# A first stage without a pool of its own on the right, with its first maxima moved and most of GpSimd's arithmetic on other engines

## The chip, the cores and the metric

The kernel runs on one core of a Trainium2 chip. The time is the device time of one launch in microseconds. TensorE multiplies matrices, VectorE, ScalarE and GpSimd work element by element, SyncE issues most of the DMAs. The kernel before takes 3284.41 us (median of three runs, 3281.88 to 3284.51).

## The reference, cut to what matters

Two layers work on 2048 tokens of width 1024, with 256 context tokens as a prefix for the first layer's keys and values. All of it is in float32.

```
h = modulate(x, shift, scale) @ w_in                 # 2464 columns: cq, ckv, kr, gates, qb, kb, vb
q_a = rms_norm(cq) @ w_uq ;  k_a, v_a = rms_norm(ckv) @ w_ukv ;  k_pe = rope(kr) ; q_pe = rope(...)
q_b, k_b = rope(rms_norm(qb)), rope(rms_norm(kb))    # 8 query heads over 2 key heads
o = softmax(q k^T * scale) v    for 8 + 8 heads, over 256 + 2048 keys
x = layer_norm(alpha * x + gate * (concat(o * silu(g)) @ w_out))
x = the second layer, a gated MLP that mixes tokens in chunks of 128, on x
```

## The kernel before, in words

Every product of two float32 matrices is made of three products of rounded halves: a value is cut into a high part (a rounded copy) and a low part (value minus copy), and high x high, low x high and high x low are added up in one bank (`mm3`, lines 187 to 189).

The kernel has three stages. `phase1` makes queries, keys, values and gates for all tokens and stores them in DRAM. `attention` goes through 16 heads in four groups of 512 queries each, in an order that is written out by hand. `phase3` makes the output projection and the second layer. This case is about `phase1` and its end.

`phase1` works in two halves: the first on the context (chunk -1) and chunks 0 and 1 of 512 tokens, the second on chunks 2 and 3. For each chunk `acts` loads the raw activations (line 107, two buffers named `xr`), modulates them on ScalarE (176), copies the high part on GpSimd (178) and subtracts the low part on VectorE (179). High and low parts lie in rings of nine buffers, where a chunk needs four of each. `weights` does the same for each weight tile: load (155), high part on GpSimd (158), low part on VectorE (159). The products then come in the order key B, value B, four query B, two compressed key/value (`C2`), keys A, values A, the rope part of the keys, three compressed queries (`C3`), and last the "uq" products that make the A queries, three weight tiles `s` of two blocks for two chunks each, every one with 9 products. Units of gate products, 24 products each, are strewn in between by a generator, `gate`; in the second half six of them are left for the end.

Around the products stand small chains. `halves` cuts the squares of a result in two (242 on ScalarE, 243 on GpSimd), `rnorm` sums them with a product (251), takes a root (253) and a reciprocal (254). `rope` multiplies by a cosine table on GpSimd (223), shuffles (224), multiplies by a sine table (225) and adds on VectorE (226). `put` cuts the result in two and stores it (217). `later_rows` computes the modulation rows of later stages on VectorE (273, 275), three pieces with each weight tile, from weights that go through the two `xr` buffers as well.

The tiles lie in a pool on the left (`sp`) and an early pool on the right (`ap`), which holds squares, tables, the context's activations, the accumulators of `later_rows`, the C2 and C3 units and the values' tiles. When the uq products are through, the early pool is closed and the attention's pool `kp` is opened in its place: two slots of keys (`k`), two of values (`v`), three of queries (`q`). Then the keys of head 0 and the first two query tiles are loaded (552), and `first_peaks` makes the maxima of the first scores: 18 products with their reductions (618, 622, 632, 635) for the first group and 10 for the second. After the 18, the row of maxima goes to DRAM (639) and comes back into a row of the query tile (552), which the first score product reads. These come amid the last gate units, in this way:

```
for i, _ in enumerate(gate):
    if half == 1 and i > 0:
        n = 9 if i < 3 else 5
        if i == 3:
            todo.pop()()          # the row of maxima comes back
        for f in todo[:n]: f()
```

In `phase1` the order on each engine is not the program's. The framework's planner goes through the instructions by priority (program order, but for those in `high_priority`) with modelled durations, gives every engine and every queue a fixed order, and puts in the waits. On the chip each engine then goes through its list in order, SyncE's list of DMA issues too.

## Time and profile before

| | |
|---|---|
| median of three runs | 3284.41 us |
| profiled execution | 3284.32 us, span 3282.5 us |
| TensorE busy | 3183.2 us (97%) |
| VectorE / ScalarE / GpSimd busy | 2501.8 / 1892.4 / 1623.6 us |
| first stage | up to about 680 us |
| mean granted clock of TensorE | 0.989 |

A busy TensorE is not TensorE at its peak, since the ends of products are modelled: a product of 512 columns is shown with 0.39 us, while such products start 0.23 us apart when they follow without a wait. The clock is given as the share of full speed that was granted.

### The profile page before, as it was taken

To read this page: it belongs to the slowest core of one execution; us is meant where nothing else is said; L and a number is where in the kernel's file an instruction comes from. 1 tells how busy PE (TensorE), PEld (TensorE's weight loads), DVE (VectorE), ACT (ScalarE), POOL (GpSimd) and SP (SyncE) were. 2 spreads that over 40 slices of the span, in tenths; PEclk is the share of its full clock that TensorE was granted. 3 is DMA by queue.
4 is the path that set the end of the run, shared out by engine and by line. 5 is a ranking of instruction groups with operands and counts; after the bars stand their busy time and mean duration, and the time that the engine had idled before them with its cause. 6 is when DMAs were issued, how large, how long until landed. Compare 5 with 4: busy or idle time off the path is not lost.

```text
span 3282.5 us, 40436 instructions
## 1 busy us (share of the span) xinstructions
PE 3183.2 (97%) x13698; PEld 2429.2 (74%) x13698; DVE 2501.8 (76%) x3685; ACT 1892.4 (58%) x3258; POOL 1623.6 (49%) x1359
## 2 busy tenths in 40 slices
PE   7999999989999999999999999999999999999998
PEld 4787677767777777777666666666788878888886
DVE  4947794578988888888999999998655764855746
ACT  3433342357777777777777777777444353353352
POOL 3312441259999999998888888874100100100000
PEclk9999999989999999999999999999999999999999
DMA  6455755543122221222111111112633533533322
GB/s 235 142 164 181 247 161 175 160 115 61 40 50 61 61 59 30 63 61 61 28 30 27 27 49 29 27 30 60 165 96 109 143 120 109 155 102 109 116 91 76
DMA packets 187056, 314.08 MB, mean 96 GB/s; under 512 B 53264, under 2 KB 79184, under 8 KB 184928
## 3 DMA queue, kind: packets, MB, share of 16 engines
q1 hardware_dynamic: 178558, 283.62, 30.6%
q0 software_dynamic: 8000, 27.81, 2.8%
q8 instruction: 108, 1.77, 0.3%
q14 instruction: 100, 0.82, 0.1%
q10 hardware_dynamic: 290, 0.07, 0.0%
HBM read 240.71 MB, written 70.73 MB: 95 GB/s over the span
## 4 chain that ended last, share of the span: by engine, by line
PE 52%; issue 11%; DMA 9%; POOL 6%; DVE 6%; ACT 2%; SPq 0%; POOLq 0%; ACTq 0%; DVEq 0%
PE s L603 14%; DMA NM<-nm 6%; PE ol L603 6%; PE oh L603 5%; PE m L603 5%; POOL sa L603 4%; PE acc L935 3%; PE acc L934 3%; PE acc L936 3%; PE acc L1031 3%; PE acc L1030 3%; PE acc L1029 3%; DVE pl L603 2%; DMA q<-NM 2%; PE ps L188 1%
## 5 line engine op out<-in xcount | busy, mean ns | idle before, releaser
L603 POOL TENSOR_TENSOR sa<-sa,ph 128x512 f32<-128x512 f32 x728 | 939.4, 1290 | 61.0 <-ACT ph L603 15.5
L603 PE MATMUL s<-q,k 96*128 96x512 f32 (+2 forms) x2880 | 875.7, 400 | 37.0 <-DMA q<-NM 18.2
L603 ACT ACTIVATE ph<-s 128x512 fp32r<-128x512 f32 x1064 | 634.4, 596 | 325.6 <-PE s L603 308.2
L603 DVE TENSOR_REDUCE mx<-m 128x1 f32<-128x512 f32 x1124 | 765.4, 683 | 60.2 <-PE m L603 56.7
L603 DVE TENSOR_TENSOR pl<-s,ph 128x512 fp32r<-128x512 f32 x1064 | 729.8, 686 | 106.2 <-ACT s L603 82.1
L603 PEld LDWEIGHTS s<-q,k 96*128 96x128 f32 (+2 forms) x2880 | 539.4, 190 | 249.8 <-DVE pl L603 35.9
L603 ACT ACTIVATE s<-s 128x512 f32<-128x512 f32 x1064 | 632.0, 594 | 0.0
L603 PE MATMUL oh<-ph,v 128*128 128x512 f32 x1152 | 455.4, 395 | 0.0
L603 PE MATMUL ol<-pl,v 128*65 128x512 f32 x1152 | 455.2, 395 | 0.0
L603 PE MATMUL m<-k,q 128*128 128x512 f32 (+1 forms) x1250 | 451.3, 377 | 0.0
L67 ACT ACTIVATE wh<-w 128x1024 fp32r<-128x1024 f32 x153 | 162.2, 1060 | 469.3 <-PE acc L936 221.3
L68 DVE TENSOR_TENSOR wl<-w,wh 128x1024 fp32r<-128x1024 f32 x153 | 187.0, 1222 | 253.0 <-ACT wh L67 252.0
L603 PEld LDWEIGHTS m<-k,q 128*128 128x128 f32 (+1 forms) x1250 | 234.8, 190 | 67.9 <-DVE mx L603 15.0
L187 PE MATMUL ps<-xh,wh 128*128 128x512 f32 (+1 forms) x640 | 248.7, 389 | 6.6 <-POOL xh L178 6.6
L603 PEld LDWEIGHTS oh<-ph,v 128*128 128x128 f32 x1152 | 218.1, 189 | 49.4
L188 PE MATMUL ps<-xl,wh 128*128 128x512 f32 (+1 forms) x640 | 249.6, 390 | 4.3 <-DVE xl L179 4.2
L189 PE MATMUL ps<-xh,wl 128*128 128x512 f32 (+1 forms) x640 | 248.3, 388 | 0.0
L603 PEld LDWEIGHTS ol<-pl,v 128*65 128x65 f32 x1152 | 157.4, 137 | 50.7 <-ACT ob L603 0.3
L158 POOL TENSOR_SCALAR wh<-wr 128x1024 fp32r<-128x1024 f32 (+1 forms) x48 | 57.4, 1197 | 225.3 <-PE ps L188 116.4
L934 PE MATMUL acc<-wh,k 128*128 128x512 f32 x384 | 153.7, 400 | 0.8 <-ACT t L998 0.8
L935 PE MATMUL acc<-wl,k 128*128 128x512 f32 x384 | 153.3, 399 | 0.0
L936 PE MATMUL acc<-wh,k 128*128 128x512 f32 x384 | 152.6, 398 | 0.0
(300 smaller groups left out, 5193.5 us busy)
## 6 DMA issues: line engine op xcount, KB each, us to landing
w<-in_wug SPq DMA_DIRECT2D x64, 512.0 KB
wr<-in_w SPq DMA_DIRECT2D x38, 512.0 KB
w<-in_e_w_out SPq DMA_DIRECT2D x32, 512.0 KB
w<-in_o_w_in SPq DMA_DIRECT2D x32, 512.0 KB
w<-in_o_w_out SPq DMA_DIRECT2D x32, 512.0 KB
wr<-in_e_w_mod SPq DMA_DIRECT2D x24, 512.0 KB
wr<-in_o_w_mod SPq DMA_DIRECT2D x24, 512.0 KB
q<-QB SPq DMA_DIRECT2D x96, 128.0 KB
```

Of the source, the lines that this page charges most:

```text
L67: e.nc.scalar.activation(h, src, AF.Copy)
L68: e.nc.vector.tensor_tensor(out=l, in0=src, in1=h.bitcast(F32), op=ALU.subtract)
L187: nc.tensor.matmul(out, lhsT=wh(k), rhs=xh(k), start=i == 0, stop=False)
L188: nc.tensor.matmul(out, lhsT=wh(k), rhs=xl(k), start=False, stop=False)
L189: nc.tensor.matmul(out, lhsT=wl(k), rhs=xh(k), start=False, stop=i == n - 1)
L603: i = getattr(self.engine, name)(*args, **kw)
L934: nc.tensor.matmul(ps[t], lhsT=h[:, ts], rhs=w[0][:, k, :], start=first, stop=False)
L935: nc.tensor.matmul(ps[t], lhsT=h[:, ts], rhs=w[1][:, k, :], start=False, stop=False)
L936: nc.tensor.matmul(ps[t], lhsT=l[:, ts], rhs=w[0][:, k, :], start=False, stop=last)
L1029: nc.tensor.matmul(ps, lhsT=w[0][:, k, :], rhs=h, start=k == 0, stop=False)
L1030: nc.tensor.matmul(ps, lhsT=w[0][:, k, :], rhs=l, start=False, stop=False)
L1031: nc.tensor.matmul(ps, lhsT=w[1][:, k, :], rhs=h, start=False, stop=k == NK - 1)
```

## The change

The early pool goes. The attention's pool `kp` is opened at the start, with a slot of its own name for each buffer: `k0`, `k1`, `v0`, `v1` (head h takes slot h % 2, as the two buffers took turns before) and three `q`. The first stage's short-lived tiles lie in these slots as boxes of several tiles, which are freed as a whole: the context's activations and the accumulators in `k0`, the tables in `v0`, the C2 and C3 units in `k1` and `v1`, the values' tiles in `q`. Squares go to `sp`. The rings of activations have eight buffers instead of nine.

The weights' high part is made by ScalarE with priority, rope's cosine product and the low half of the squares by VectorE. GpSimd keeps the activations' high parts (178), the sums of squares (384, 454) and the small sets of ones.

The keys and queries of the first head are loaded ahead of the uq products of the second half, whose order is now 2, 0, 1, so that the ropes come first; the values are loaded ahead of the second of them, into the slot where the tables were. Eight of the first maxima follow the units of the last two, one each, and the other twenty come amid the gate units, five each; the row comes back ahead of the maxima behind the third.

```diff
+    kp = e.kp = e.stay.enter_context(tc.tile_pool(name="kv", bufs=1, side="right", reuse_waits="tile"))
+    def box(tag, n, dtype=F32):
+        t = kp.tile([P, n, CH], dtype, name="box" + tag, tag=tag, bufs=1)
+        return [t[:, i, :] for i in range(n)]
...
-            nc.gpsimd.tensor_scalar(out=h[:, :n], in0=w[:, :n], scalar1=1.0, scalar2=0.0, op0=ALU.mult, op1=ALU.add)
-            nc.vector.tensor_tensor(out=l[:, :n], in0=w[:, :n], in1=h[:, :n].bitcast(F32), op=ALU.subtract)
+            with tc.high_priority():
+                nc.scalar.activation(h[:, :n], w[:, :n], AF.Copy)
+                nc.vector.tensor_tensor(out=l[:, :n], in0=w[:, :n], in1=h[:, :n].bitcast(F32), op=ALU.subtract)
...
-            pool, bufs = (ap, 4) if c < 0 else (sp, 9)
+            ctx = box("k0", 8, F32R) if c < 0 else None
...
+                    h, l = (sp.tile([P, 2, n], F32R, name="x" + q, tag="x" + q, bufs=8) for q in "hl")
...
-            nc.gpsimd.tensor_tensor(out=u, in0=t, in1=C[:m], op=ALU.mult)
+            nc.vector.tensor_tensor(out=u, in0=t, in1=C[:m], op=ALU.mult)
...
+            tabs = box("v0", 4)
...
-            nc.gpsimd.tensor_tensor(out=o[:, 1, :], in0=sq, in1=o[:, 0, :].bitcast(F32), op=ALU.subtract)
+            nc.vector.tensor_tensor(out=o[:, 1, :], in0=sq, in1=o[:, 0, :].bitcast(F32), op=ALU.subtract)
...
+            def unit():
+                if not units:
+                    units.extend(box("k1", 8, F32R) + box("v1", 4, F32R))
+                    del units[taken:]
...
-            for s in range(3):
+            if half == 1:
+                assert not aside
+                flush()
+                e.first = [keys(e, 0, 1), [queries(e, 0, g) for g in range(2)]]
+                todo = first_peaks(e, sp, pp)
+            for s in (2, 0, 1):
+                if half == 1 and s == 0:
+                    e.first[0] = keys(e, 0, 2, e.first[0])
...
+                        if half == 1 and s != 2:
+                            todo.pop(0)()
                     flush()
-            if half == 1:
-                assert not aside
-                flush()
-                early.close()
-                e.kp = e.stay.enter_context(tc.tile_pool(name="kv", bufs=2, side="right", reuse_waits="tile"))
-            if half == 1:
-                e.first = keys(e, 0), [queries(e, 0, g) for g in range(2)]
-                todo = first_peaks(e, sp, pp)
             for i, _ in enumerate(gate):
-                if half == 1 and i > 0:
-                    n = 9 if i < 3 else 5
-                    if i == 3:
+                if half == 1:
+                    n = 5
+                    if i == 2:
                         todo.pop()()
```

`keys` takes `parts`: 1 loads the keys alone, 2 the values alone.

## Rows read from the trace of the kernel before

**Rows 1.** Two stretches: length; busy PE, PEld, DVE, ACT, POOL; clock; DMA share; GB/s.
```profile
385.00:460.00 75.00, 69.63 (x301) 54.68 (x300) 74.94 (x80) 30.99 (x50) 35.15 (x25) 1.00 0.48 144
635.00:680.00 45.00, 34.58 (x126) 23.67 (x124) 18.06 (x33) 5.29 (x8) 4.31 (x4) 0.84 0.82 196
```
**Rows 2.** Waits of TensorE up to 760 us: total, times, longest.
```profile
PE ss L251 <- ACT oq L242: 10.1, 5, 6.3
PE s L603 <- DMA q<-NM: 8.9, 1, 8.9
PE ss L251 <- POOL oq L243: 7.6, 10, 2.3
PE ps L187 <- POOL xh L178: 6.6, 2, 4.3
```
**Rows 3.** TensorE in order of time at the end of the first stage.
```profile
665.05 6.25 PE L618 MATMUL m<-k,q 96*128 96x512 f32 x10
...
680.20 1.62 PE L603 MATMUL s<-q,k 97*128 97x512 f32 x3 [8.89 <-DMA q<-NM]
```
**Rows 4.** Chain of waits: three scores soon after the start, and later.
```profile
683.95 1.28 PE s L603 x3
...
690.74 0.70 PE s L603 x3
```
**Rows 5.** SyncE in order of time at the end of the first stage.
```profile
635.43 0.68 SPq L552 DMA_DIRECT2D k<-KA  x1
...
638.55 10.07 SPq L552 DMA_DIRECT2D q<-QN  x1
...
666.90 0.37 SPq L639 DMA_DIRECT2D NM<-nm  x1
...
676.84 0.24 SPq L552 DMA_DIRECT2D q<-NM  x1
```
**Rows 6.** Groups by line and shape, GpSimd to 640 us; ScalarE's from the page.
```profile
L158 POOL TENSOR_SCALAR wh<-wr 128x1024 fp32r<-128x1024 f32 x42 | 52.2, 1244 | 203.8 <-PE ps L188 98.1 <-PE ps L189 35.1 <-DMA wr<-in_w 30.6
L223 POOL TENSOR_TENSOR t<-t,tc 128x512 f32<-128x512 f32 x28 | 40.5, 1446 | 90.3 <-DVE t L323 24.4 <-ACT t L353 24.3 <-issue 14.5
L243 POOL TENSOR_TENSOR oq<-sq,oq 128x512 fp32r<-128x512 f32 x28 | 39.4, 1407 | 19.7 <-ACT oq L242 19.5
...
L67 ACT ACTIVATE wh<-w 128x1024 fp32r<-128x1024 f32 x153 | 162.2, 1060 | 469.3 <-PE acc L936 221.3
```
**Rows 7.** Groups by line and shape, VectorE and GpSimd in 400 to 460 us.
```profile
L225 DVE TENSOR_TENSOR sq<-sq,ts 128x512 f32<-128x512 f32 x8 | 8.5, 1057 | 0.0
L68 DVE TENSOR_TENSOR oo<-t,oo 128x512 fp32r<-128x512 f32 x7 | 7.3, 1038 | 0.0
...
L223 POOL TENSOR_TENSOR t<-t,tc 128x512 f32<-128x512 f32 x9 | 13.0, 1442 | 30.3 <-DVE oo L68 7.4 <-DVE t L323 6.9 <-DVE sq L225 6.0
L243 POOL TENSOR_TENSOR oq<-sq,oq 128x512 fp32r<-128x512 f32 x8 | 11.0, 1381 | 0.8 <-ACT oq L242 0.7
```
**Rows 8.** VectorE in order of time: one operation without and with GpSimd beside it.
```profile
428.78 0.68 DVE L225 TENSOR_TENSOR sq<-sq,ts 128x512 f32<-128x512 f32 x1
...
436.21 1.52 DVE L225 TENSOR_TENSOR sq<-sq,ts 128x512 f32<-128x512 f32 x1
```
**Rows 9.** GpSimd, SyncE, ScalarE and TensorE in order of time between the halves.
```profile
356.40 1.29 POOL L223 TENSOR_TENSOR t<-t,tc 128x512 f32<-128x512 f32 x1 [3.18 <-ACT t L482]
...
360.81 3.48 POOL L178 TENSOR_SCALAR xh<-xr 128x1024 fp32r<-128x1024 f32 x2
...
366.59 0.38 SPq L107 DMA_DIRECT2D xr<-in_xT  x1
...
372.20 1.52 ACT L176 ACTIVATE xr<-xr,md 128x512 f32<-128x512 f32 x2 [3.89 <-DMA xr<-in_xT]
...
374.90 0.80 PE L187 MATMUL ps<-xh,wh 128*128 128x512 f32 x1 [4.27 <-POOL xh L178]
```
**Rows 10.** ScalarE in order of time before the last gates of the first half.
```profile
309.04 0.81 ACT L176 ACTIVATE xr<-xr,md 128x512 f32<-128x512 f32 x1 [7.27 <-DMA wr<-in_uq]
```

More of the change, by code (lines that the diff above doesn't have):

```diff
@@ L87, in exact @@
         def exact(shape, name, src):
-            t = ap.tile(shape, F32, name=name + "0", tag="sq", bufs=4)
+            t = sp.tile(shape, F32, name=name + "0", tag="sq", bufs=4)
             nc.sync.dma_start(t, src)
@@ L121, in phase1 @@
                                      start=kk + k == 0, stop=kk + k == 4)
-            mrow = ap.tile([2, CH], F32, name="mrow", tag="sq", bufs=4)
+            mrow = sp.tile([2, CH], F32, name="mrow", tag="sq", bufs=4)
             nc.scalar.activation(mrow, ps[:2, :], AF.Copy)
@@ L126, in phase1 @@
             if j == 2:
-                raw = {(-1, kk): raws(-1, kk, "xl", 9) for kk in range(4)}
+                raw = {(-1, kk): raws(-1, kk, "xl", 8) for kk in range(4)}
                 wpre = []
                 for i in range(2):
-                    w = sp.tile([P, 1024], F32, name="wr", tag="xh", bufs=9)
+                    w = sp.tile([P, 1024], F32, name="wr", tag="xh", bufs=8)
                     nc.sync.dma_start(w.rearrange("p (k f) -> p k f", k=NK), I["w1"][i])
                     wpre.append(w)
-        raw.update({(0, kk): raws(0, kk, "xl", 9) for kk in range(4)})
+        raw.update({(0, kk): raws(0, kk, "xl", 8) for kk in range(4)})
         md = cp.tile([P, 2, 16], F32, name="md")
@@ L172, in acts @@
                 r = raw[c, kk] if (c, kk) in raw else raws(c, kk)
-                h = pool.tile([P, 2, n], F32R, name="xh", tag=tag + "h", bufs=bufs)
-                l = pool.tile([P, 2, n], F32R, name="xl", tag=tag + "l", bufs=bufs)
+                if c < 0:
+                    h, l = (ctx[2 * kk + i].rearrange("p (a t) -> p a t", a=2) for i in range(2))
+                else:
+                    h, l = (sp.tile([P, 2, n], F32R, name="x" + q, tag="x" + q, bufs=8) for q in "hl")
                 for k in range(2 * kk, 2 * kk + 2):
@@ L209, in tmp @@
         def tmp(m, n, tag, bufs=2):
-            return (ap if tag == "sq" else sp).tile([P, CH], F32, name=tag, tag=tag, bufs=bufs)[:m, :n]
+            return sp.tile([P, CH], F32, name=tag, tag=tag, bufs=bufs)[:m, :n]
         def put(y, dst):
@@ L230, in tables @@
             r = {}
+            tabs = box("v0", 4)
             for c in chunks:
-                C = ap.tile([P, CH], F32, name="tc", tag="tc", bufs=2)
-                S = ap.tile([P, CH], F32, name="ts", tag="ts", bufs=2)
+                C, S = tabs[:2]
+                del tabs[:2]
                 nc.sync.dma_start(C, I["cos" + name][:, c * CH:(c + 1) * CH])
@@ L261, in later_rows @@
         def later_rows(r0):
-            acc, bias = {}, []
+            acc, room = {}, []
             def add(r, k):
@@ L268, in add @@
                 if k == 0:
-                    acc[r] = [ap.tile([P, CH], F32, name="acc", tag="xc" + "hl"[r % 2], bufs=4) for i in range(2)]
+                    acc[r] = room[:2] if room else None
+                    if not room:
+                        room.extend(box("k0", 4))
+                        acc[r] = room[:2]
+                    del room[:2]
                 for i in range(2):
@@ L368, in phase1 @@
                 aside, rate = later_rows(2), 3
-            unit = lambda: tuple(ap.tile([P, CH], F32R, name="c" + q, tag="c" + q, bufs=6) for q in "hl")
+            units, taken = [], 4 * len(xs)
+            def unit():
+                if not units:
+                    units.extend(box("k1", 8, F32R) + box("v1", 4, F32R))
+                    del units[taken:]
+                u = units[:2]
+                del units[:2]
+                return u
             ts, sqs, C2 = {}, {}, {}
@@ L440, in phase1 @@
                 aside, rate = later_rows(0), 3
+            taken = 12
             C3 = {}
@@ L507, in ring @@
 def ring(e, last):
-    g = [e.kp.tile([P, 8, CH], F32R, name="k", tag="k", bufs=2), e.kp.tile([P, 4, CH], F32R, name="v", tag="v", bufs=2)]
+    g = [e.kp.tile([P, 8, CH], F32R, name="k", tag="k%d" % last, bufs=1), e.kp.tile([P, 4, CH], F32R, name="v", tag="v%d" % last, bufs=1)]
     g += [spare(e) for u in range(2)] if last else [e.carry.tile([P, 2, CH], F32R, name="xc", tag="xc", bufs=1)]
@@ L552, in load, with keys @@
     e.nc.sync.dma_start(dst.bitcast(F32), src)
-def keys(e, h):
+def keys(e, h, parts=3, KV=None):
     nc = e.nc
-    K = e.kp.tile([P, 2, NT], F32R, name="k", tag="k", bufs=2)
-    V = e.kp.tile([P, NTT, 2 * DV + 2], F32R, name="v", tag="v", bufs=2)
-    if h < NH:
+    turn = h % 2 if h < NH else h // 4 % 2
+    K, V = KV or (None, None)
+    if parts & 1:
+        K = e.kp.tile([P, 2, NT], F32R, name="k", tag="k%d" % turn, bufs=1)
+    if parts & 2:
+        V = e.kp.tile([P, NTT, 2 * DV + 2], F32R, name="v", tag="v%d" % turn, bufs=1)
+    if parts < 3:
+        if parts == 1:
+            load(e, K[:NOPE], e.KA[:, h * NOPE:(h + 1) * NOPE, :].rearrange("s p t -> p s t"))
+            load(e, K[NOPE:NOPE + ROPE], e.KR.rearrange("s p t -> p s t"))
+            nc.gpsimd.memset(K[NOPE + ROPE:NOPE + ROPE + 1, 0, :].bitcast(F32), 1.0)
+            return K, V
+        load(e, V[:, :, :2 * DV], e.VA[h])
+    elif h < NH:
         load(e, K[:NOPE], e.KA[:, h * NOPE:(h + 1) * NOPE, :].rearrange("s p t -> p s t"))
```

7 lines of the change are left out of this document (2 added, 5 removed).

## The prediction, made before the change was run

> **What bounds the kernel now.** I read the slices of the page first: TensorE is busy 97% of the span, so time can only come from the places where it waits, runs at half clock, or is fed slowly. The stages by window come next: in 385 to 460 us VectorE is busy 74.9 of 75 us beside a TensorE that is busy 69.6, and in 635 to 680 us TensorE is busy only 34.6 of 45 us at a mean granted clock of 0.84 [rows 1]. Then the waits of TensorE up to 760 us, which is where the change is: 10.1 us for ScalarE's first half of the squares (one of them 6.3), 8.9 us for the row of maxima, 7.6 us in ten waits for GpSimd's second half of the squares, and 6.6 us for GpSimd's activations [rows 2]. The attention and the last stage are not touched: their tiles get other names in the same two slots and the written-out order is the same. So I work on the first 680 us and let the rest stand.
>
> The largest loss is where the first stage hands over to the attention. There the reader is to see a chain. SyncE issues the load of the keys at 635.43, after the early pool is closed, and the load of the first queries waits 10.07 us, to 648.6 [rows 5]. By then TensorE has gone through nearly all remaining gate products, so that the maxima come last and alone: the last ten products take 6.25 us, 0.62 each, because each waits for VectorE's reduction [rows 3]. The maxima go out at 666.90, are read back from 676.84, and the first score starts at 680.20 after 8.89 us of idling [rows 3, 5]. It starts at half clock: three scores take 1.28 us there and 0.70 later, 0.43 and 0.23 a product [rows 4].
>
> **The sum, part by part.** The profiled execution took 3284.32 us, 1.8 more than its span of 3282.5, and 0.1 below the median of 3284.41; I sum against 3284.3.
>
> *First maxima amid the last products.* What goes: the 8.9 us wait; the slow feeding, ten products at 0.62 instead of 0.23 (3.9 us) and eight before them at the same pace (about 3.1 us); the 15 products up to about 686.6 us (four groups of scores, three maxima) at 0.43 instead of 0.23 (2.9 us). Together 18.8. Will it be covered? The keys' tile now lies in a slot that is free once the modulation rows are out, so keys and queries can be asked for before the last uq products, and nothing of the early pool has to close. Eight maxima lie between uq units of 9 products (2.1 us each, against about 0.6 of VectorE), five behind each of the first two gate units. After the row is sent there remain four gate units of 24 products and ten maxima: 106 products x 0.23 = 24 us. The round trip is 9.9 us to the read and 3.4 to the score, 13.3 [rows 5, 3], so 11 us are left over. Behind SyncE's wait for that row stand stores of gates and loads that the first scores don't need. What is late next is the handover itself: ScalarE must leave the gates' function for the exponential and banks must come free. I bound it by zero and by the 2.9 us that half clock costs now, and take 1.4, in the middle. Term: -17.4, and at least -6 if the row still comes late.
>
> *GpSimd's arithmetic moved.* 48 copies of weights (42 of 1024 columns at 1.24 us, six shorter), 32 rope products (28 of 128 rows at 1.45) and 30 low halves (28 of full width at 1.41) leave GpSimd [rows 6]. The copies go to ScalarE, where the same shape takes 1.06 us in the last stage [rows 6]: some 50 us over 650, on an engine that is busy 31 of 75 us in the fullest stretch [rows 1]. I cost them at nothing; if the cover is gone they cost what a blocked ScalarE queue costs (below). The 62 products and low halves go to VectorE. The nearest rows are the same shape, once alone at 0.68 us and once at 1.52 beside GpSimd [rows 8]; I take 0.68, since what ran beside it leaves. That is 62 x 0.68 = 42 us more work in 650, or 94 at the upper bound.
>
> Against that stands what VectorE loses to GpSimd now. In 400 to 460 us the table products take 1.06 us on average and the stores' low halves 1.04 [rows 7], against 0.68 alone [rows 8]: eight and seven of them lose 5.5 us. Other kinds in that stretch lose less, and I add 2 as an estimate. The 9 rope products and 8 low halves of GpSimd there [rows 7] add 17 x 0.68 = 11.6. So the stretch grows by 11.6 - 7.5 = 4 us of VectorE, which has no idle time in it, and TensorE has 5.4 us of its own in 385 to 460 [rows 1]. Elsewhere VectorE has idle time. Bounds: 0 if TensorE's idle time swallows it, +12 if nothing is won back; I take +2.
>
> The Trainium skill, "SBUF — State Buffer", section "SBUF: two separate sides", says that VectorE with two SBUF inputs and GpSimd take turns on one pair of ports, each for a whole instruction. The 0.68 against 1.52 agrees with it. By that rule taken alone the moved work would cost VectorE nothing on balance, and the sum would be 2 us lower.
>
> In return TensorE no longer waits for GpSimd's low halves: 7.6 us in ten waits, and 3.8 of the 10.1 us for ScalarE's halves, leaving out the longest [rows 2]. VectorE's queue takes GpSimd's place, and a reciprocal in front is longer than the old product was. Bounds: -11.4 to +6 (ten waits of 0.6 more each); I take -4.
>
> *Eight buffers instead of nine, and a free GpSimd at the turn of the halves.* At 360.81 GpSimd converts two tiles of the fourth chunk late: from 356.40 on, ropes and a weight copy lie in front. So the last raw tile is asked for at 366.59, ScalarE gets it at 372.20, and TensorE waits 4.27 us at 374.90 and goes on at half clock [rows 9]. With ten products at 0.2 more I put the whole at 6.3 us. With GpSimd free these conversions can begin at about 356, while the last gate product of the first half lets go of its tiles one by one. But with eight buffers the chunk's first tile, too, has to wait for that, so two raw tiles are fetched late instead of one. The fetch (366.59 to 372.20), ScalarE's two passes and GpSimd's copy take 8.3 us to 374.90 [rows 9]. The two fetches may go out at about 359 and 360.5, when the tiles in front are subtracted, so the last tile would be ready near 369 to 370, some 5 us earlier than now; I keep 2 us of wait for the second of them. Term: -4; bounds -6.3 (no wait) and +6 (both fetches held up on SyncE as the one is now).
>
> *Left as it is.* The 6.3 us wait stays: at 309.04 ScalarE stands 7.27 us at a raw tile whose fetch is late behind the modulation rows on SyncE, with the squares' copy queued behind it [rows 10]. Nothing in the change moves those fetches. I take 0; it could vanish with another order (-10, with its half-clock products). Table loads, boxes for short-lived tiles, and the keys' and values' loads cost nothing on TensorE: each box is rewritten long after its readers (C2 and C3 take turns a whole phase apart), and the values' load waits only for ropes that are now done first. If this cover failed, SyncE would stand with the stores behind it: a few us, within the range.
>
> Sum: -17.4 + 2 - 4 - 4 = -23.4, that is 3284.3 - 23.4 = 3260.9; I say **3261**.
>
> **Rivals.**
> 1. *The other stalls go too.* With fewer collisions the planned order holds, and the waits of rows 2 vanish largely: -18.8 at the handover, -11.4, -6.3 and half of the 10 = -41.5, with VectorE swallowed: 3243. For it: most of these waits have GpSimd behind them. Against: the 6.3 has not.
> 2. *The maxima still come last.* The queries' load may again wait for a product, or SyncE may be held by stores in front of it; the planner then fills TensorE with gate products as now. This is also the case in which the change doesn't do what it says. Then at most -6 of the 18.8 is won: 3284.3 - 6 - 4 + 2 = 3276, and 3282 with nothing from the small terms. For it: the 10.07 us at 638.55 wait for a TensorE product that the queries don't use [rows 5]. Against: in the new place nothing of an early pool has to close first.
> 3. *VectorE becomes the bound in the query stretches.* If nothing is won back, 11.6 us in the second half and as much of the first half as has no slack, say half: +17 instead of +2, and the low halves at +6 instead of -4: 3286 with the handover won. For it: no idle time in 75 us.
> 4. *ScalarE's queue blocks (slower).* The 48 weight copies wait for a fetch or for a free slot, and now squares, evacuations and oq copies stand behind them. The one such block seen, 7.27 us at 309.04, cost TensorE 6.3 us and, with the half-clock products after it, some 10 [rows 10, 2]. Each further block costs the same, so from three on the gain is gone: 3261 + 3 x 10 = 3291, and slower by the bound below. For it: a copy with priority goes to the front of the queue whenever the planner believes that its data is there. Against: in the last stage 153 such copies run on ScalarE.
>
> **Chances.** The forecast 0.55 (its own range 3250 to 3272), rival 1 0.20, rival 2 0.10, rival 3 0.08, rival 4 0.07. About 0.2% of the time, 6.6 us, is what a measurement of this kernel can tell from no change, so faster is below 3277.8. Faster: 0.55 + 0.20 + 0.06 of rival 2 + 0.03 of rival 3 = 0.84. Same: 0.04 + 0.04 + 0.02 of rivals 2, 3 and 4 = 0.10. Slower: 0.06. The range runs from 3236 (part of rival 1 below it) to 3282 (rival 2 within, rivals 3 and 4 mostly above).
>
> **What would show it.** Right: the wait of the first score for the row of maxima is gone or under 2 us, products of maxima lie between uq and gate products, and the first score starts near 660 us; GpSimd shows only activations' copies and sums before 650 us; VectorE's table products there take 0.68; the wait at the turn is under 3 us. Wrong: a block of maxima at the end as now (rival 2), new waits of TensorE for VectorE's oq in 385 to 460 us (rival 3), or ScalarE idle at weight copies with TensorE waiting behind (rival 4). The forecast is wrong if the start of the scores moves by less than 12 us or by more than 35, or if the time after it changes at all.

## The result, and the profile after

The changed kernel takes 3238.74 us (median of 4 runs, 3233.69 to 3241.65) against 3284.46 for the kernel before (4 runs, 3281.88 to 3288.09): a ratio of 0.9863, 95% interval 0.9851 to 0.9875. That is 45.7 us less, where 23 were forecast. The time lies in the range, but it is rival 1's size rather than the forecast's, and a quarter of the gain came from a stage that I had let rest. The profiled execution took 3241.65, with a span of 3239.8.

TensorE is now busy 3162.1 of 3239.8 us. The page's first part:

```profile
PE 3162.1 (98%) x13698; PEld 2422.8 (75%) x13698; DVE 2492.7 (77%) x3747; ACT 1935.2 (60%) x3306; POOL 1477.3 (46%) x1249
```

The two stretches that answer to [rows 1] are below (the second has moved forward with the end of the first stage). In the first, TensorE has no gap left, with 331 products instead of 301; VectorE is still nearly full; GpSimd does nothing at all. In the second, where 10 us were lost, TensorE is busy 44.58 of 45 us at a clock of 0.98.

```profile
385.00:460.00 75.00, 75.00 (x331) 60.61 (x330) 73.95 (x92) 36.45 (x55) 0.00 (x0) 1.00 0.48 153
605.00:650.00 45.00, 44.58 (x191) 35.45 (x190) 18.15 (x29) 7.73 (x13) 2.15 (x2) 0.98 0.84 202
```

The waits of TensorE up to 760 us answer to [rows 2]. The first line is the start of the kernel and was there before. The wait of the first score for the row of maxima (8.9) is gone; so is that for GpSimd's low halves (7.6). The 10.1 for ScalarE's half, of which I had wanted to leave 6.3 standing, is 2.3.

```profile
PE ps L124 <- DMA wr<-in_e_w_mod: 7.2, 1, 7.2
PE ps L193 <- DVE oo L68: 4.1, 3, 2.2
PE ps L194 <- DVE xl L185: 3.4, 6, 1.3
PE ss L258 <- DVE oq L250: 3.0, 2, 2.4
PE ps L193 <- POOL xh L184: 2.9, 2, 1.8
PE ss L258 <- ACT oq L249: 2.3, 2, 1.9
```

The end of the first stage, TensorE and then SyncE in order of time, answers to [rows 3, 5]. The keys are asked for at 525.42 instead of 635.43 and the queries' load waits for nothing; the first maximum runs at 580.59; the row goes out at 627.62, is read from 639.40, and the first score starts at 649.70 instead of 680.20, with no idle time in front of it. The scores start at full pace: three take 0.87 from the first start to the last end, where the first three took 1.62 before [rows 3]. A stretch at half pace is left, but earlier and shorter: from 603 to 606 us, behind two waits for VectorE (0.83 and 0.70), the granted clock is 0.50, the lower of its two levels, and nine products of the uq stretch start some 0.43 us apart (first fence below, columns as in [rows 1]). The next loss is new and small, 1.02 us at the tenth product of the scores, for VectorE's pl.

```profile
603.00:606.00 3.00, 3.00 (x9) 2.35 (x8) 1.91 (x4) 0.00 (x0) 0.00 (x0) 0.50 0.99 336
```
```profile
580.59 0.87 PE L651 MATMUL m<-k,q 96*128 96x512 f32 x3
...
649.70 0.87 PE L636 MATMUL s<-q,k 97*128 97x512 f32 x3
...
653.68 0.96 PE L636 MATMUL s<-q,k 97*128 97x512 f32 x3 [1.02 <-DVE pl L636]
```
```profile
525.42 1.01 SPq L574 DMA_DIRECT2D k<-KA  x1
...
537.39 0.60 SPq L574 DMA_DIRECT2D q<-QN  x1
...
627.62 0.36 SPq L672 DMA_DIRECT2D NM<-nm  x1
...
639.40 0.25 SPq L574 DMA_DIRECT2D q<-NM  x1
```

VectorE in 400 to 460 us, by line and shape, answers to [rows 7]: with nothing beside it on GpSimd, the table product takes 0.688 us instead of 1.057, the stores' low half 0.685 instead of 1.038, and the squares' low half, new here, 0.671.

```profile
L231 DVE TENSOR_TENSOR sq<-sq,boxv 128x512 f32<-128x512 f32 x7 | 4.8, 688 | 0.0
L250 DVE TENSOR_TENSOR oq<-sq,oq 128x512 fp32r<-128x512 f32 x7 | 4.7, 671 | 0.0
L68 DVE TENSOR_TENSOR oo<-t,oo 128x512 fp32r<-128x512 f32 x6 | 4.1, 685 | 0.0
```

**Where the 43 us of the two spans are.** I cut both traces at the same counts of TensorE's products, in order of their start times: the 2200th product of the first stage, the first score, the first product of the last stage, the start of the last one. In the first stage only the products that write a `ps` bank are counted, here and in the stretches below; where the order of the products differs, the same count need not be the same product.

| stretch | before | after | difference |
|---|---|---|---|
| start to 2200th product | 582.8 | 564.7 | -18.1 |
| 2200th product to first score | 97.4 | 85.0 | -12.4 |
| attention | 1632.4 | 1631.1 | -1.3 |
| last stage | 956.8 | 945.9 | -10.9 |

The last line was a surprise: TensorE has the same products in the same order there, and its waits are nearly the same. What differs is the spacing of products. Over a 40 us window of the last stage that has the same products in it, TensorE starts 173 of them before and 178 after, at full clock and without a gap in both (columns: stretch, length, busy and count, clock, DMA share, GB/s):

```profile
2415.00:2455.00 40.00, 40.00 (x173) 1.00 0.30 92
```
```profile
2382.00:2422.00 40.00, 40.00 (x178) 1.00 0.32 93
```

Over the whole stage the mean distance from one 512-column product to the next, stalls over 0.3 us left out, is 233.3 ns before and 230.7 after; 2.6 ns times some 3850 products is 10 us.

### The profile page after: what moved, and what is told of

It reads as the page before. It is cut to its first block, busy times and chain, and to the rows that moved or that the text cites. A ratio compares the mean times of both kernels' runs of the same rounds, so it can differ in the third digit from the quotient of the medians.

```text
span 3239.8 us, 40308 instructions
## 1 busy us (share of the span) xinstructions
PE 3162.1 (98%) x13698; PEld 2422.8 (75%) x13698; DVE 2492.7 (77%) x3747; ACT 1935.2 (60%) x3306; POOL 1477.3 (46%) x1249
## 4 chain that ended last, share of the span: by engine, by line
PE 59%; DMA 13%; issue 12%; POOL 8%; DVE 7%; ACT 2%; SPq 0%; POOLq 0%; ACTq 0%; DVEq 0%
PE s L636 12%; DMA NM<-nm 7%; POOL sa L636 6%; PE ol L636 5%; PE ps L193 4%; PE ps L194 4%; PE ps L195 4%; PE oh L636 4%; PE m L636 4%; PE acc L967 3%; PE acc L968 3%; PE acc L969 3%; PE acc L1064 3%; PE acc L1062 3%; PE acc L1063 3%
## 5 line engine op out<-in xcount | busy, mean ns | idle before, releaser
L636 POOL TENSOR_TENSOR sa<-sa,ph 128x512 f32<-128x512 f32 x728 | 939.1, 1290 | 60.3 <-ACT ph L636 14.5
L636 PEld LDWEIGHTS m<-k,q 128*128 128x128 f32 (+1 forms) x1250 | 234.3, 189 | 67.5 <-DVE mx L636 14.5
L194 PE MATMUL ps<-xl,wh 128*128 128x512 f32 x608 | 238.4, 392 | 3.4 <-DVE xl L185 3.4
L193 PE MATMUL ps<-xh,wh 128*128 128x512 f32 x608 | 238.5, 393 | 2.9 <-POOL xh L184 2.9
L195 PE MATMUL ps<-xh,wl 128*128 128x512 f32 x608 | 237.8, 391 | 0.0
L194 PEld LDWEIGHTS ps<-xl,wh 128*128 128x128 f32 x608 | 114.6, 188 | 29.9 <-DVE xl L185 6.0
```

The costliest lines, as they stand in the source:

```text
L193: nc.tensor.matmul(out, lhsT=wh(k), rhs=xh(k), start=i == 0, stop=False)
L194: nc.tensor.matmul(out, lhsT=wh(k), rhs=xl(k), start=False, stop=False)
L195: nc.tensor.matmul(out, lhsT=wl(k), rhs=xh(k), start=False, stop=i == n - 1)
L636: i = getattr(self.engine, name)(*args, **kw)
```

## The experiments

Twelve experiments were run, e1 with the kernel before itself. Each ratio is to the kernel before, measured beside it on the same chip, where its median was 3282.06 to 3284.46. The stage times are from one profiled execution of each, which lies up to 6 us from the median (e4 and e8 below it, e7 above).

| kernel | time, us | ratio, 95% interval | to 2200th | to first score | attention | last stage | spacing there, ns |
|---|---|---|---|---|---|---|---|
| before | 3284.46 | | 582.8 | 97.4 | 1632.4 | 956.8 | 233.3 |
| after | 3238.74 | 0.9863 (0.9851 to 0.9875) | 564.7 | 85.0 | 1631.1 | 945.9 | 230.7 |
| e1 before again | 3288.81 | one run | 585.6 | 96.8 | 1631.8 | 959.8 | 233.4 |
| e2 slots only | 3273.19 | 0.9970 (0.9957 to 0.9982) | 583.9 | 96.7 | 1629.9 | 951.2 | 230.7 |
| e3 engines only | 3264.54 | 0.9946 (0.9931 to 0.9961) | 562.5 | 99.8 | 1631.9 | 955.5 | 233.3 |
| e4 engines undone | 3261.94 | 0.9939 (0.9923 to 0.9955) | 581.2 | 85.2 | 1629.3 | 946.3 | 230.7 |
| e5 late maxima | 3236.99 | 0.9861 (0.9846 to 0.9876) | 562.3 | 84.9 | 1630.5 | 944.6 | 230.8 |
| e6 even places | 3240.28 | 0.9868 (0.9854 to 0.9883) | 562.5 | 84.8 | 1625.6 | 950.3 | 231.9 |
| e7 odd places | 3247.50 | 0.9891 (0.9876 to 0.9906) | 562.1 | 85.8 | 1627.1 | 961.5 | 233.3 |
| e8 even and order | 3241.86 | 0.9877 (0.9861 to 0.9894) | 562.7 | 84.4 | 1623.2 | 950.8 | 232.0 |
| e9 same in 256 | 3224.22 | 0.9829 (0.9815 to 0.9842) | 562.0 | 84.7 | 1625.1 | 936.2 | 227.4 |
| e10 copies back | 3257.49 | 0.9926 (0.9912 to 0.9939) | 584.5 | 84.9 | 1629.0 | 943.9 | 230.7 |
| e11 halves back | 3249.61 | 0.9901 (0.9887 to 0.9914) | 574.3 | 85.1 | 1629.3 | 945.3 | 230.8 |
| e12 boxes only | 3236.42 | 0.9856 (0.9839 to 0.9872) | 566.3 | 80.4 | 1628.2 | 946.6 | 230.8 |

**The theory I began with** was the table of differences: three causes that add up, the engine moves, the early maxima, and the place of the attention's tiles in SBUF. The rivals were that the first two are one (a late weight copy delays all that follows it), and that the last stage's gain is chance from run to run.

### e1, the kernel before, once more

No edit.

> The kernel before, unchanged, profiled a second time. In the last stage (from the first output product to the end) TensorE's products followed each other every 233.3 ns before and every 230.7 after the change, 10 of the 43 us between the two profiled executions, though no line of that stage changed. Theory (the place of the attention's tiles sets this pace): 233.3 again, within 0.4, and that stage 957 us again within 2. Rival (the pace differs from one execution to the next): another value, 230 to 234, and a stage that is 3 to 11 us off. The first 680 us: the wait of 8.9 us for the row of maxima and the one of 6.3 us for ScalarE's half of the squares again, by both.

The two large waits are there again, at 8.4 us and at 10.8 in five, 6.9 the longest, and the spacing is 233.4. The last stage took 959.8, outside the 2 us that I had allowed: at the same spacing it has some 3 us more of stalls, so a difference of that size in this stage between two profiles shows nothing.

```profile
PE ss L251 <- ACT oq L242: 10.8, 5, 6.9
PE s L603 <- DMA q<-NM: 8.4, 1, 8.4
```

Over all profiles in the table the spacing never moves by more than 0.1 ns between kernels with the same places: it belongs to the kernel, not to the run.

### e2, the tiles' places alone

The kernel before, with the keys', values' and last stage's tiles in slots of their own name (the last stage's lines are left out here):

```diff
...
-    K = e.kp.tile([P, 2, NT], F32R, name="k", tag="k", bufs=2)
-    V = e.kp.tile([P, NTT, 2 * DV + 2], F32R, name="v", tag="v", bufs=2)
+    turn = h % 2 if h < NH else h // 4 % 2
+    K = e.kp.tile([P, 2, NT], F32R, name="k", tag="k%d" % turn, bufs=1)
+    V = e.kp.tile([P, NTT, 2 * DV + 2], F32R, name="v", tag="v%d" % turn, bufs=1)
```

> The kernel before with one edit: keys and values get the slots k0, v0, k1, v1 by name, as in the change, so that in the attention and the last stage they lie where the change puts them; the first stage, its pool, its engines and the place of the first maxima are as before. Theory (place sets the pace): the last stage takes 947 us instead of 957, pace 230.7 ns, and the time falls by 8 to 11 us, to about 3275. Rival (execution to execution): 3284 within 3, pace not tied to it. Both: the first 680 us as before within 2.

The spacing falls to 230.7 and the time by 0.3%, with nothing changed in what is computed, in which order or by which engine; 4 us of other stalls came in the last stage. In the first stage nothing is gained; its two large waits, in the view of TensorE's waits up to 760 us, stand much as in [rows 2]:

```profile
PE s L604 <- DMA q<-NM: 8.4, 1, 8.4
PE ss L251 <- ACT oq L242: 7.4, 3, 5.7
```

So new names for the slots do not free the handover, as long as an early pool has to close first.

### e3 and e4, the three engine moves alone, and all but them

e3 is the kernel before with these lines; e4 the changed kernel with them taken back.

```diff
-            nc.gpsimd.tensor_scalar(out=h[:, :n], in0=w[:, :n], scalar1=1.0, scalar2=0.0, op0=ALU.mult, op1=ALU.add)
-            nc.vector.tensor_tensor(out=l[:, :n], in0=w[:, :n], in1=h[:, :n].bitcast(F32), op=ALU.subtract)
+            with tc.high_priority():
+                nc.scalar.activation(h[:, :n], w[:, :n], AF.Copy)
+                nc.vector.tensor_tensor(out=l[:, :n], in0=w[:, :n], in1=h[:, :n].bitcast(F32), op=ALU.subtract)
...
-            nc.gpsimd.tensor_tensor(out=u, in0=t, in1=C[:m], op=ALU.mult)
+            nc.vector.tensor_tensor(out=u, in0=t, in1=C[:m], op=ALU.mult)
...
-            nc.gpsimd.tensor_tensor(out=o[:, 1, :], in0=sq, in1=o[:, 0, :].bitcast(F32), op=ALU.subtract)
+            nc.vector.tensor_tensor(out=o[:, 1, :], in0=sq, in1=o[:, 0, :].bitcast(F32), op=ALU.subtract)
```

> The kernel before with the engine moves alone: weights' high parts on ScalarE with priority, rope's cosine product and the low half of the squares on VectorE; pools, nine buffers, and the late maxima as before. Theory (GpSimd's collisions and its place in the chains cost the first stage its waits): the last square sum falls from 591 to about 575 us, the waits for GpSimd's low halves (7.6 us) and for its activations (6.6) are gone or under 3 each, the handover wait of 8.9 us stays; 3284 - 16 = 3268, 3262 to 3273. Rival (the gain of the first 580 us is from the pool and the order 2, 0, 1): 3284 within 4. VectorE as the bound (rival 3 of the prediction): 3287 to 3295.

> The changed kernel with the three engine moves taken back to GpSimd; slots, eight buffers, order 2, 0, 1 and the early maxima stay. Theory: the 16 us of the first 580 us come back, the handover stays without its wait, the last stage stays at its faster pace: 3239 + 16 = 3255, 3250 to 3260. Rival (pool and order made that gain): 3239 within 4. If the handover depends on the engines too, 3262 to 3270.

With the moves alone the 2200th product comes 20.3 us earlier (562.5 for 582.8) and the handover is as bad as it was: the wait for the row is 9.8. Without them it comes at 581.2 and the handover takes 85.2, as in the changed kernel. In these profiles the two parts are nearly independent: -20 and -12 to -14. The medians are less tidy: e3 gains 17.5 us and e4 20.1, of which 10 are the last stage's, together 8 less than the change; e4's four runs spread over 9.4 us. In e3 the wait for ScalarE's half of the squares, which I had left standing, is no longer among the waits; in e4 it is still there (8.0 in three). TensorE's waits up to 760 us in e3, then in e4:

```profile
PE s L604 <- DMA q<-NM: 9.8, 1, 9.8
PE ss L252 <- DVE oq L244: 2.8, 2, 2.4
```
```profile
PE ss L257 <- ACT oq L248: 8.0, 3, 4.9
```

ScalarE's order in time shows how that wait went. In the kernel before (first fence, with GpSimd's line ahead) the squares' sum is ready at 302.98, but its copy comes at 309.76, behind the late raw tile of [rows 10]. In e3 (second fence) ScalarE still stands 5.17 us at that tile, but the copy runs ahead of it:

```profile
301.27 1.71 POOL L454 TENSOR_TENSOR sq<-sq 128x512 f32<-128x512 f32 x1 [2.20 <-ACT sq L448]
...
309.76 0.61 ACT L242 ACTIVATE oq<-sq 128x512 fp32r<-128x512 f32 x1
```
```profile
299.56 0.63 ACT L243 ACTIVATE oq<-sq 128x512 fp32r<-128x512 f32 x1 [0.89 <-POOL sq L455]
305.37 1.52 ACT L177 ACTIVATE xr<-xr,md 128x512 f32<-128x512 f32 x2 [5.17 <-DMA xr<-in_xT]
```

### e5 and e12, the maxima where they were, and the uq order too

e5 is the changed kernel with the loads of keys and queries and the first maxima written behind the last uq products, as before; e12 has the uq products in the old order as well.

```diff
...
-            if half == 1:
...
-                e.first = [keys(e, 0, 1), [queries(e, 0, g) for g in range(2)]]
-                todo = first_peaks(e, sp, pp)
             for s in (2, 0, 1):                # e12: for s in range(3)
...
-                        if half == 1 and s != 2:
-                            todo.pop(0)()
+            if half == 1:
...
+                e.first = keys(e, 0), [queries(e, 0, g) for g in range(2)]
+                todo = first_peaks(e, sp, pp)
...
```

> The changed kernel with its engine moves, boxes and product order kept, but the keys and queries asked for, and the first maxima computed, where the kernel before does it: behind the last uq products. Theory (the early maxima are worth what the stage table says, 12 to 13 us between the 2200th product of the first stage and the first score): the stretch is 97 to 100 us instead of 85.0, the first score waits 8 to 10 us for the row of maxima again, the time is 3250 to 3253. Rival A (free slots alone are enough: with no early pool to close, the loads go out in time and the maxima need not come early): the wait is under 2 us, the time 3238 to 3242. Rival B (my forecast's 17.4 for this step): 3256.

> The kernel with late maxima (loads and first maxima written where the kernel before has them) with the uq products too in the order of the kernel before in both halves, 0, 1, 2. What is left of the change is the engine moves, the boxes with eight buffers, and the attention's tiles by name. Theory (the free tiles alone do it: with nothing to close, the planner brings loads and maxima forward by itself): no wait for the row of maxima, 85 us from the 2200th product to the first score, the start of the scores at 645 to 652, the time 3235 to 3242. Rival (with ropes last, the stores of the queries come late and the loads with them: the order 2, 0, 1 is what frees the handover): a wait of 4 to 10 us for the row of maxima, that stretch 90 to 98 us, the time 3244 to 3252. In the first half the turn of the halves (1344th to 1472nd product) should be 38 us again, as in the kernel with even places and that order, and the stretches on either side of it 33.5 and 31.

My theory lost to its rival in e5: 3237 us, a handover of 84.9, no wait. e12 shows the same with the old order of products. In e12 the 1856th to the 2200th product take 85.1 instead of 81.6, and the handover 80.4; together they are as in the changed kernel (165.5, and 166.6). What is left of the change at the handover is that the tiles lie in slots that are free when their turn comes (and eight buffers for nine). Then the planner brings loads and maxima forward by itself: in e12, SyncE asks for the keys at 529.86 although the line stands behind the uq products. TensorE's longest waits up to 760 us show none for the row, and SyncE's loads and the row, in order of time, come within 5 us of the changed kernel's:

```profile
PE ps L193 <- POOL xh L184: 4.2, 2, 2.2
PE ps L194 <- DVE xl L185: 4.2, 5, 1.8
PE ss L258 <- DVE oq L250: 3.5, 2, 2.5
```
```profile
529.86 0.68 SPq L570 DMA_DIRECT2D k<-KA  x1
...
631.38 0.38 SPq L668 DMA_DIRECT2D NM<-nm  x1
...
640.73 0.26 SPq L570 DMA_DIRECT2D q<-NM  x1
```

### e6 and e7, tiles shifted by 32 to 96 bytes

Where the build places a tile is known from its layout, so I could set the start of every product against the places of its operands. Products were 227 ns apart where the moving rows and the weights of the product behind them started alike modulo 64 bytes, and 234 where they did not. Whether it is the next product's weights or its own is not shown. The two nearly always lie alike, and the few products at a change of tiles do not settle it: in the changed kernel 62 of them, unlike their own weights and like the next, take 229.2, and 55, like their own and unlike the next, 232.4; counted modulo 256, the unit that comes out below, the same two groups take 230.4 (83) and 232.7 (90), and in e9 it is the other way round, 233.3 (32) and 231.7 (44). The two kernels try the rule:

```diff
-        V = e.kp.tile([P, NTT, 2 * DV + 2], F32R, name="v", tag="v%d" % turn, bufs=1)
+        V = e.kp.tile([P, NTT * (2 * DV + 2) + 12], F32R, name="v", tag="v%d" % turn, bufs=1)
+        V = V[:, :NTT * (2 * DV + 2)].rearrange("p (t d) -> p t d", t=NTT)
```

That is e7. e6 has `+ 12 + 8 * turn` in this place, and 32 bytes more ahead of the first stage's tiles and on either side of the carried Z tile.

> The changed kernel with its tiles shifted by 32 to 96 bytes, nothing else: two values' tiles made 32 to 80 bytes longer, 32 bytes put ahead of the first stage's tiles, 32 on either side of the carried Z tile. Theory (a 512-column product takes some 227 ns when its moving rows and the weights loaded behind it, those of the next product, start at the same place modulo 64 bytes, and some 234 when they are 32 bytes apart): all 3935 such products of the last stage are now alike in this, where 1834 are 32 bytes apart in the changed kernel, and in the first stage 445 fewer are apart. So the mean spacing in the last stage goes from 230.7 to 227.5, the last stage from 945.9 to about 934, the first stage is 2 us shorter, the time is 3222 to 3227. Rival (what counts is where in SBUF a tile lies, for example above byte 188000, or which tile it is beside): a shift of under 100 bytes changes nothing, spacing 230.7, time 3237 to 3242.

> The changed kernel with two values' tiles 48 bytes longer and nothing else, which puts all key, value and query tiles 32 bytes from where the last stage's weights start, modulo 64 (3800 of its 3935 products). Theory: the spacing in the last stage goes up from 230.7 to 234, the last stage to about 958; the first stage is 2 us shorter, since its boxes now agree with its own weights; the time is 3247 to 3251. Rival (the address itself): as the changed kernel, 230.7 and 3237 to 3242. The two kernels together: the theory has them 24 us apart in the last stage, the rival 0.

e7 came out as the theory had it: 233.3 ns in the last stage, which takes 961.5, the time slower than the changed kernel's by 9. e6 did not: 231.9 instead of 227.5. So the address itself is not what counts (a shift of under 100 bytes moves the stage by 4 to 16 us), but 64 is not the unit. Split by the distance of the two places modulo 256, the last stages of the kernels so far agree but for one group (groups of under 50 products left out):

| distance mod 256 | 0 | 64 | 128 | 192 | 32, 96, 160, 224 |
|---|---|---|---|---|---|
| mean spacing, ns | 227.6 | 229.2 | 232.5 to 232.9 | 233.4 | 232.9 to 234.1 |
| kernel (products) | after (1919) | e6 (868) | e6 (1195, 973) | e6 (648) | before, after, e7 (nearly all the rest) |

The group that does not fit is the kernel before's: it has some 440 products at distance 0 too, in short runs between others, and they take 229.7. In its first stage, though, 1732 products at distance 0 are 227.6 apart, although both places are odd multiples of 32: alike is what counts, not any alignment.

### e9, alike modulo 256

```diff
-        V = e.kp.tile([P, NTT, 2 * DV + 2], F32R, name="v", tag="v%d" % turn, bufs=1)
+        V = e.kp.tile([P, 2432 + 40 * turn], F32R, name="v", tag="v%d" % turn, bufs=1)
+        V = V[:, :NTT * (2 * DV + 2)].rearrange("p (t d) -> p t d", t=NTT)
...
-    g += ... else [e.carry.tile([P, 2, CH], F32R, name="xc", tag="xc", bufs=1)]
+    g += ... else [e.carry.tile([P, 2 * CH + 128], F32R, name="xc", tag="xc", bufs=1)[:, 88:2 * CH + 88].rearrange("p (a t) -> p a t", a=2)]
...
+        cp.tile([P, 8], F32, name="pad1")
```

> The changed kernel with its tiles shifted by up to 864 bytes, nothing else, so that in every 512-column product of the last stage the moving rows start at the same place modulo 256 bytes as the weights of the product behind it (and the boxes of the first stage too). The kernels with even and odd places gave 232.5 ns a product at a difference of 128 (modulo 256), 229.2 at 64, 233.4 at 192, 233 to 234 at odd multiples of 32; the changed kernel 227.6 at 0 and 234 at 96 and 160. Theory (only a difference of 0 modulo 256 gives full speed): the last stage's mean goes from 230.7 to 227.5, its length from 945.9 to 932 to 934 us; the first stage gains 2; the time is 3222 to 3228, below both kernels. Rival (it is not the difference, but something else of the place, such as which tiles share a part of SBUF): anything from 229 to 233.5 in the last stage, 3235 to 3250.

The spacing is 227.4 and the time 3224.22 us, below the changed kernel's interval and the fastest here. The last stage is 936.2, not 932 to 934: 13 us come from the spacing, and some 3 are given back in stalls over 0.3 us. A few more come in the attention, 1623 to 1627 in the four kernels with shifted tiles against 1628 to 1631 in the others with the attention's tiles by name; its spacing hardly moves (232.7 for 232.9), its gaps over 0.3 us add up to 100 to 105 us in the four and to 104 to 113 in the others, and I have no cause for it. 40 us of the last stage, with the same products as above, in e6, e7 and e9 (one fence each, columns as above):

```profile
2375.00:2415.00 40.00, 40.00 (x174) 1.00 0.29 92
```
```profile
2378.00:2418.00 40.00, 40.00 (x174) 1.00 0.30 92
```
```profile
2375.00:2415.00 40.00, 40.00 (x178) 1.00 0.35 106
```

The counts are 174, 174 and 178. The changed kernel has 178 here as well, but only where one of its two sets of tiles is read; e9 has the pace with both. e2 shows that the unit is 256 and not a multiple of it: in its layout 1246 products of the last stage lie at a distance of 256 modulo 512 and take 227.2, and 672 at 0 modulo 512 take 228.4.

### e8, the order of the uq products in the first half

e6 with `for s in ((2, 0, 1) if half else (0, 1, 2))`.

> The kernel with even places, and in the first half the uq products in the order of the kernel before (0, 1, 2 instead of 2, 0, 1), since in the changed kernel the stretch of the 1216th to the 1344th product took 37.5 us, with waits for VectorE's oo tiles, and 33.5 with the engine moves alone. Theory: that stretch goes back to 33.5 and the time is 4 us below the kernel with even places, 3218 to 3223, the fastest so far. Rival (the stretch is long for the boxes or the eight buffers): the stretch stays at 37 and the two kernels take the same time.

The stretch from the 1216th to the 1344th product goes back to 33.5, as expected, but the time does not fall. The turn of the halves behind it (1344th to 1472nd product) goes from 32.0 back to 38.5, and the 1728th to 1856th from 34.9 to 31.1. So the gain at the turn, 39.0 to 31.6 in the changed kernel, is the order's, and the order takes it back on either side. e12, with eight buffers, a free GpSimd and the old order, has 38.7 there, with TensorE waiting for GpSimd's x halves as in [rows 9]:

```profile
365.58 0.79 PE L193 MATMUL ps<-xh,wh 128*128 128x512 f32 x1 [2.25 <-POOL xh L184]
```

### e10 and e11, single engine moves taken back

e10 is the changed kernel with the weight copies on GpSimd again, and they and the subtractions behind them without priority (the two were not tried apart); e11 the one with the squares' low halves on GpSimd again.

> The changed kernel with one of its three engine moves taken back: the weight copies are GpSimd's again, at no special priority. With all three taken back the time was 3261.9, 23 above. Theory (my prediction's: the copies are hidden wherever they stand, and what GpSimd held up was the low halves and the ropes): 3239 to 3245, little lost. Rival (the copies were what kept GpSimd from the x halves and the low halves, and late weights held TensorE up in the first half and at the table stretch): most of the 23, 3250 to 3260, with the waits for xh and for the squares back.

> The changed kernel with only the low halves of oq given back to GpSimd. Theory of the prediction (ten waits of TensorE for them, 7.6 us, and the ScalarE half left as it was): 4 to 8 us lost, 3243 to 3247, by waits ss<-oq for GpSimd. Rival A (with copies and ropes gone from GpSimd its queue is free and it is in time): under 2 us lost. Rival B (it is the larger part of the 23): 3250 or more.

Without the move of the copies 18.8 us of the 23.2 are lost (3257.49 for 3238.74, where e4 has 3261.94); without that of the low halves, 10.9. They overlap. e10 came out at the rival's time but not by the waits that it named, and e11 lies between its expectation (3243 to 3247) and its rival (3250 or more). In e10 TensorE waits mainly for VectorE, not for GpSimd. The stretch from the 1472nd to the 1728th product takes 77.6 us instead of 63.1, more than the 69.3 of before, and VectorE is busy in all 77.5 of it. Two things are seen there. With five of GpSimd's copies in that stretch, single operations of VectorE take 1.40 to 1.53 us that take 0.69 to 0.75 without, as in [rows 8]; four of them make some 3 us. And VectorE does 93 instructions there instead of 74: in this kernel's order more of its work falls into the stretch. How the 14.5 us divide between the two was not tried apart. TensorE's waits up to 760 us in e10, then in e11, and between them two of VectorE's operations in e10 in order of time:

```profile
PE ss L257 <- DVE oq L249: 12.7, 11, 4.1
PE ps L194 <- DVE wl L163: 4.7, 3, 3.1
```
```profile
401.88 1.53 DVE L230 TENSOR_TENSOR sq<-sq,boxv 128x512 f32<-128x512 f32 x1
...
414.64 1.53 DVE L68 TENSOR_TENSOR oo<-t,oo 128x512 fp32r<-128x512 f32 x1
```
```profile
PE ps L193 <- DVE oo L68: 8.3, 3, 6.7
PE ss L258 <- POOL oq L250: 5.2, 11, 1.0
```

In e11 the low halves cost 5.2 us in waits of their own, near the 4 that I had priced; the rest of the 10.9 comes by another way, in waits for the ropes' stores (8.3, where the changed kernel has 4.1), and in a turn of the halves of 38.9 for 31.6. How much of either is the planner's other order and how much GpSimd's time was not tried apart.

## Why the prediction was right and wrong, step by step

**First maxima amid the last products: right in size, half right in cause.** Forecast -17.4, measured -12.4 to the first score and -1.1 over the first sixty scores. The signs that I named came: no wait, maxima between uq and gate products, a row whose read is issued 10 us before the first score. The first scores run at full pace (0.87). What is late next is VectorE, where the step had named ScalarE and the banks, bounded by 2.9 and taken at 1.4: it makes two maxima wait 1.1 us, a uq product 0.7 and the tenth product of scores 1.0, after which three groups of four products take 1.19, 1.20 and 1.05 us instead of 0.93. With the half pace from 603 to 606 us, which costs some 1.5 as an estimate (eight products at 0.42 instead of 0.23), that is enough for the 4 us that are missing. But the cause in the step's name is not it: e5 and e12 give the same handover with the maxima written where they were. The sentence that held was "nothing of the early pool has to close".

**GpSimd's arithmetic moved: mis-sized by 15 us and more.** The terms +2 for VectorE, -4 for the low halves, and 0 for the copies sum to -2; e3 measures -20.3 up to the 2200th product. Three steps failed. "I cost them at nothing" priced the copies by what they cost ScalarE: e10 prices the move, its priority included, at -18.8. By which way it gains that is shown for some 3 us only (four operations of VectorE held up by GpSimd's copies). "So the stretch grows by 4 us of VectorE" had the parts right and the whole wrong. The table products and low halves did fall to 0.69 each. But between the 1472nd and the 1728th product VectorE now does 7 reciprocals instead of 9 and 74 instructions instead of 71, 13 of them new (7 table products of the cosine, 6 low halves): its old work is not tied to that stretch, and part of it is done in others. So TensorE became the bound there, 63.0 busy of 63, and the stretch went from 69.3 to 63.1. And "the 6.3 us wait stays" failed: with the engine moves alone it is gone (e3), without them it stays (e4), though the late fetch to which I had traced it is still there in e3 (5.17 us of ScalarE). What went is the squares' place in ScalarE's queue behind it. My reading of [rows 10] took the fetch for the cause, where the order of the queue made TensorE wait; that order came out another way with the engine moves, and by which of them is not shown.

**The turn of the halves: right in size for a wrong reason.** Forecast -4, measured -7.4. But eight buffers and a free GpSimd leave it at 38.7 (e12); the order of the uq products moves it, and pays for it elsewhere, so the term is worth nothing.

**"The attention and the last stage are not touched": failed by 10.9 us.** The order and the engines are the same there, and I took that for the same time. The tiles' addresses changed, and e2, e7 and e9 show that these set the spacing. I had named the failure ("if the time after it changes at all"), but no rival had it.

**Rivals.** Rival 1 (the other stalls go too) is nearest: its -11.4 and -6.3 came for the most part (the waits for the squares' halves fall from 17.7 us to 5.3), and a part of its 10. That its 3243 is so near to 3239 is luck: without the last stage's 11 us, which it did not have, the change gains 35 us and not its 41.5. Rival 2 fell with the wait; rival 3 with 75.0 busy us of 75 on TensorE; rival 4 with ScalarE's 36.45 busy of 75 and 1.1 us in all of VectorE's waits for weight copies in that stretch. The likeliest case was right in its mechanism at the handover only; two of the other gains, 20 and 11 us, are larger than what I gave them, so that the time lies 3 us inside the range's lower end by luck. The upper end leaned on a slip: rival 2's 3282 does not come out of its terms, where 6 us less than 3284.3 is 3278.

## What to carry to other kernels

Where a planner orders the work, ask what keeps a tile from being free, not where its line stands: releasing the slot moved 12 us, moving the line nothing. Price an engine that is relieved by whoever stands behind its results, and not by the waits that name it. And when a kernel lives on TensorE's spacing, lay out the moving tiles and the weights so that they start alike modulo 256 bytes, and look whether the spacing falls: in the attention it did not. A change of names or sizes can set it or lose it in a stage that nobody edited.

## What the runs showed of the hardware

In the first and the last stage of these kernels, the product behind a 512-column product starts 227 ns after it when the moving rows start at the same place modulo 256 bytes as the weights, after 229 at a distance of 64, and after 232.5 to 234 at nearly every other that was seen. Places alike modulo 256 but not modulo 512 are as fast (227.2, e2). Between e7 and e9 the spacing makes 21 of the 25 us by which the same products differ in a stage that TensorE fills (961.5 and 936.2); the rest is in stalls over 0.3 us. In the attention, where several kinds of products alternate, the rule does not hold: some 2000 products at distance 0 modulo 256 are 233 apart in the changed kernel, and some 2800 are 234 apart in e9. There something else sets the pace, and these runs don't show what.
